# A decoder step: the down projection's middle groups in seven products, with the weights' sums made in DRAM by transfers

## The chip, the cores and the metric

The kernel is one program on one core of a Trainium2 chip. Five engines work side by side and wait for one another by semaphores: TensorE (PE, with its weight loads as PEld), VectorE (DVE), ScalarE (ACT), GpSimd (POOL) and SyncE (SP), which here only issues transfers. Sixteen DMA engines move the data between DRAM and the on-chip memory. The metric is the device time of one execution, in microseconds (us).

## The reference, cut to what matters

One layer is applied to 576 tokens (512 of a prompt and 64 of eight samples), each a vector of 1024, all in float32.

```python
h = rmsnorm(x, g_pre_mix)
z = h @ w_in                      # gated linear attention, retention, gates
m = mixers(z) @ w_mix_out         # chunked recurrences, two branches of 4 heads
x = x + rmsnorm(m, g_post_mix)
mk, mv = rmsnorm(mem) @ w_xk, rmsnorm(mem) @ w_xv     # 256 memory tokens
x = x + rmsnorm(cross_attn(rmsnorm(x), mk, mv, w_xq, w_xo), g_post_xa)
hf = rmsnorm(x, g_pre_ffn)
x = x + rmsnorm(square(relu(hf @ w_up)) @ w_down, g_post_ffn)   # hidden width 4096
```

The change is in the last line, and in what loads `x` and `mem` at the start.

## The kernel before

**Float32 in three matmuls.** Activations lie with features on the partitions and the tokens in two halves of 288 columns. Every float32 operand is split into a high part in a reduced format (`fp32r`, a ScalarE copy, L94) and a low part, the rest (a VectorE subtraction, L95); a product of two tiles takes the three matmuls high by high, low by high and high by low (L251 to L253 in `mm3`, L281 in `sevenfold`).

**Weights.** A list `plan` holds every weight tile in the order of use, 128 rows of 1024 (512 KB). `wfetch` (L172) has SP load the next one into a ring of six `wraw` buffers; `wsplit` makes `wh` and `wl` from it (rings of three); `wnext` keeps two split tiles ahead of TensorE. `gemm_m` takes one tile and makes 48 matmuls, 24 for each half of the tokens.

**Order.** First the memory's keys and values, while `xnorm` loads and normalizes the tokens; then eight mixer units, one for each head of each branch (`unit` in `mixers`): eight `gemm_m` each (q, k, two for v, four for gates), between whose halves `tick()` advances side chains written as generators: scores, attention and states of the same unit. A chain's step `attend` ends in a norm whose power is taken on GpSimd (`rs`, L887), and two steps later `turn` (L1029) transposes the normed tile on TensorE. Then come the output projection, the cross-attention and the feed-forward part. Each engine executes its own instructions strictly in the order in which they stand in its queue; the framework lays these orders down when the program is built, and sets the semaphore waits by the tiles that are read and written.

**Feed-forward.** The hidden width is cut into four groups `g` of 1024. Group 0 is made plainly. In groups 1 to 3 the up projection goes by `sevenfold`: for each of four blocks of 256 hidden columns the product is a 2 by 2 by 2 product of blocks (input halves, output halves, token halves), and a scheme of the Strassen and Winograd kind makes it with seven block products of 12 matmuls instead of eight. Its sums of activations (`fsh`, `fsl`) are made once, and the sums of weights by VectorE for each block (`begin`, four subtractions `minus` at L213, in the buffers of the ring and a separate buffer `wq`). The down projection of every group is plain: eight `gemm_m`, whose results are added onto `y3` (L734 copies the first group's, L761 adds the next two groups', and `last` ends with the fourth). `sevenfold`'s results pass through relu and square on ScalarE (L714 to L724) and are split into `hh` and `hl`.

Of the kernel before, what the change touches and what calls it, by code (L numbers as in the profile page):

```python
# [13 lines left out]
P = 128  # L14
# [12 lines left out]


RING, STAY, RAW, SEVEN = 0, 1, 2, 3
# [29 lines left out]
def decoder_step(ctx, tc, xT, memT, ktc, vc, s_gla, s_ret, w_in, w_ga, w_a2, w_mix, w_xq, w_xk, w_xv, w_xo,  # L59
                 w_up, w_ups, w_down, vecs, cst, gam, y_out, mk_out, mv_out, sg_p, sr_p, sg_s, sr_s):  # L60
# [122 lines left out]
    def wsplit():
        if units:
            units.pop(0)()
        elif raws:
            if raws[0][1] == SEVEN:
                begin()
                return
# [4 lines left out]
            pool = staying[-1] if mode == STAY else wp  # L194
            wh = pool.tile([P, 1024], F32R, name="wh")
            wl = pool.tile([P, 1024], F32R, name="wl")
            split(wh, wl, raw)
            ready.append((wh, wl))

    def halves(w):  # L200
        return w.rearrange("p (q n) -> p q n", q=2)

    def begin():


        while len(raws) < 2:
            wfetch()
        p0, p1 = (raws.pop(0)[0] for _ in range(2))
        t = wp.tile([P, 1024], F32, name="wraw", bufs=N_RAW)
        q0, q1, qt = halves(p0), halves(p1), halves(t)  # L210

        def minus(out, a, b):
            nc.vector.tensor_tensor(out=out, in0=a, in1=b, op=ALU.subtract)  # L213

        def ring(raw):
            wh = wp.tile([P, 1024], F32R, name="wh")
            wl = wp.tile([P, 1024], F32R, name="wl")
            split(wh, wl, raw)
            ready.append((wh, wl))

        def own(raw, o, n):
# [1213 lines left out]
```

## Time and profile before

| what | value |
|---|---|
| median of 3 runs | 1197.8 us (1197.7 to 1197.8) |
| the profiled execution's own time | 1200.96 us |
| span of the profiled execution, first to last instruction | 1199.2 us |
| TensorE busy / its weight loads | 1168.2 us (97%) / 1134.6 us (95%) |
| VectorE / ScalarE / GpSimd busy | 747.2 us / 564.1 us / 152.7 us |
| mean granted clock of TensorE | 0.99 of full speed |

Busy times of engines are shares of the span. Matmuls overlap in their pipeline, so the length of a stage, not the duration of one matmul, says what a matmul costs. Idle time of an engine that is not the bottleneck costs nothing.

### The profile page before, as it was taken

To read this page: it belongs to the slowest core of one execution; us is meant where nothing else is said; L and a number is where in the kernel's file an instruction comes from. 1 tells how busy PE (TensorE), PEld (TensorE's weight loads), DVE (VectorE), ACT (ScalarE), POOL (GpSimd) and SP (SyncE) were. 2 spreads that over 40 slices of the span, in tenths; PEclk is the share of its full clock that TensorE was granted. 3 is DMA by queue.
4 is the path that set the end of the run, shared out by engine and by line. 5 is a ranking of instruction groups with operands and counts; after the bars stand their busy time and mean duration, and the time that the engine had idled before them with its cause. 6 is when DMAs were issued, how large, how long until landed. Compare 5 with 4: busy or idle time off the path is not lost.

```text
span 1199.2 us, 22007 instructions
## 1 busy us (share of the span) xinstructions
PE 1168.2 (97%) x9022; PEld 1134.6 (95%) x9022; DVE 747.2 (62%) x1334; ACT 564.1 (47%) x993; POOL 152.7 (13%) x165
## 2 busy tenths in 40 slices
PE   8999999999999999999999989999999999999995
PEld 7899999999999999999999878889999999999995
DVE  6756657566746574757777545686937546456565
ACT  5534546443444344524564534556527416515652
POOL 0521213122312231221001000000000000000000
PEclk9999999999999999999999999999999999999998
DMA  8762424232424232422745677653223223321631
GB/s 291 244 213 89 128 80 137 75 125 88 128 71 143 74 128 89 128 89 76 231 130 159 226 233 238 222 164 123 88 71 105 89 71 103 109 71 56 217 108 60
DMA packets 65621, 157.98 MB, mean 132 GB/s; under 512 B 5648, under 2 KB 34576, under 8 KB 65392
## 3 DMA queue, kind: packets, MB, share of 16 engines
q1 hardware_dynamic: 65520, 156.57, 41.0%
q8 instruction: 71, 1.16, 0.4%
q14 instruction: 30, 0.25, 0.1%
HBM read 140.29 MB, written 16.25 MB: 131 GB/s over the span
## 4 chain that ended last, share of the span: by engine, by line
PE 89%; DVE 4%; DMA 2%; ACT 2%; issue 1%; POOL 1%; SPq 0%; POOLq 0%; DVEq 0%; ACTq 0%
PE psg L251 22%; PE psg L252 22%; PE psg L253 22%; PE psa L281 6%; PE psg L281 3%; PE psa L251 2%; PE pso L281 2%; PE psa L252 1%; PE psa L253 1%; DMA wraw<-in_w_xo 1%; PE pso L1254 1%; DVE wl L95 1%; PE psa L1097 1%; PE pso L1092 1%; DVE res L527 1%
## 5 line engine op out<-in xcount | busy, mean ns | idle before, releaser
L251 PE MATMUL psg<-xh,wh 128*128 128x288 f32 x1280 | 381.5, 298 | 0.4 <-DVE t L819 0.3
L252 PE MATMUL psg<-xh,wl 128*128 128x288 f32 x1280 | 377.9, 295 | 0.8 <-DVE wl L95 0.8
L253 PE MATMUL psg<-xl,wh 128*128 128x288 f32 x1280 | 377.8, 295 | 0.0
L95 DVE TENSOR_TENSOR wl<-wraw,wh 128x1024 fp32r<-128x1024 f32 x196 | 241.8, 1234 | 93.0 <-ACT wh L94 92.3
L94 ACT CAST wh<-wraw 128x1024 fp32r<-128x1024 f32 x196 | 206.0, 1051 | 187.5 <-PE psg L253 105.7
L251 PEld LDWEIGHTS psg<-xh,wh 128*128 128x128 f32 x1280 | 240.8, 188 | 3.5 <-issue 2.2
L252 PEld LDWEIGHTS psg<-xh,wl 128*128 128x128 f32 x1280 | 240.9, 188 | 1.1 <-DVE wl L95 1.0
L253 PEld LDWEIGHTS psg<-xl,wh 128*128 128x128 f32 x1280 | 240.6, 188 | 0.1
L251 PE MATMUL psg<-hh,wh 128*128 128x288 f32 x512 | 152.2, 298 | 0.7 <-DVE y L761 0.6
L252 PE MATMUL psg<-hh,wl 128*128 128x288 f32 x512 | 150.6, 295 | 0.3 <-DVE wl L95 0.3
L253 PE MATMUL psg<-hl,wh 128*128 128x288 f32 x512 | 150.7, 295 | 0.0
L251 PEld LDWEIGHTS psg<-hh,wh 128*128 128x128 f32 x512 | 96.1, 188 | 1.6 <-issue 1.1
L252 PEld LDWEIGHTS psg<-hh,wl 128*128 128x128 f32 x512 | 96.0, 188 | 0.6 <-DVE wl L95 0.6
L253 PEld LDWEIGHTS psg<-hl,wh 128*128 128x128 f32 x512 | 96.1, 188 | 0.0
L333 POOL TENSOR_TENSOR rs<-ms,mhalf 96x3 f32<-96x3 f32 (+1 forms) x11 | 11.0, 999 | 525.1 <-DVE ms L326 525.1
L955 ACT COPY vt<-psg 128x512 f32<-128x512 f32 x16 | 9.4, 587 | 77.5 <-PE psg L253 77.5
L887 POOL TENSOR_TENSOR rs<-mv,mhalf 128x1 f32<-128x1 f32 x48 | 29.8, 621 | 112.7 <-DVE mv L882 64.6
L957 DVE COPY vd<-psg 128x128 f32<-128x128 f32 x32 | 7.8, 286 | 55.6 <-ACT vt L955 55.6
L251 PE MATMUL psg<-bh,wh 128*128 128x288 f32 x128 | 38.4, 300 | 1.6 <-ACT wh L94 1.1
L252 PE MATMUL psg<-fh,wl 128*128 128x288 f32 x128 | 38.9, 304 | 1.0 <-DVE wl L95 1.0
L655 DVE TENSOR_TENSOR y<-psg,y 128x576 f32<-128x576 f32 x16 | 12.1, 757 | 44.4 <-PE psg L253 44.4
L251 PE MATMUL psg<-fh,wh 128*128 128x288 f32 x128 | 39.0, 305 | 0.2 <-ACT fh L94 0.2
(331 smaller groups left out, 2413.0 us busy)
## 6 DMA issues: line engine op xcount, KB each, us to landing
wraw<-in_w_in SPq DMA_DIRECT2D x64, 512.0 KB, 3.7
wraw<-in_w_down SPq DMA_DIRECT2D x38, 512.0 KB, 4.3
wraw<-in_w_ups SPq DMA_DIRECT2D x24, 512.0 KB, 3.7
wraw<-in_ktc SPq DMA_DIRECT2D x16, 512.0 KB, 5.0
wraw<-in_vc SPq DMA_DIRECT2D x16, 512.0 KB, 4.5
wraw<-in_w_xq SPq DMA_DIRECT2D x14, 512.0 KB, 4.3
wraw<-in_w_xo SPq DMA_DIRECT2D x14, 512.0 KB, 6.4
wraw<-in_w_up SPq DMA_DIRECT2D x14, 512.0 KB, 4.5
```

Source lines behind the costliest of these rows:

```text
L94: nc.scalar.copy(hi, src)
L95: nc.vector.tensor_tensor(out=lo, in0=src, in1=f32(hi), op=ALU.subtract)
L251: nc.tensor.matmul(out, ah, bh, start=first, stop=False)
L252: nc.tensor.matmul(out, al, bh, start=False, stop=False)
L253: nc.tensor.matmul(out, ah, bl, start=False, stop=last)
L281: nc.tensor.matmul(out, s[:, q, k], m[:, k], start=first and k == i == 0, stop=k == 3 and i == 2, skip_group_check=True)
L527: nc.vector.tensor_tensor(out=res[:, kk, c], in0=y[:, kk], in1=rj, op=ALU.add)
L655: nc.vector.tensor_tensor(out=out, in0=a, in1=b, op=op)
L887: nc.gpsimd.tensor_tensor(out=rs[:t], in0=mv[:t], in1=mhalf[:t, 0:1], op=ALU.pow)
L1092: nc.tensor.matmul(so[32 * j:32 * j + 8, o], qsd[:, b * 8:b * 8 + 8], s0[:, j], start=False, stop=True, skip_group_check=True, tile_positi ...
L1097: nc.tensor.matmul(U[:, j * 256:(j + 1) * 256], kst[g][:, 2 * bp + j, :], vst[g], start=True, stop=True)
L1254: nc.tensor.matmul(acc[rows, :256], x(h), w[:, h], start=first, stop=last, skip_group_check=True, tile_position=(0, 32 * h))
```

## The change

It has three parts.

1. In groups 1 and 2 the down projection too goes by `sevenfold`, in four blocks of seven products (argument `xh7`). For that the hidden activations are kept as `ha` (two quarters), `fh[:, 2]` (one) and four sums of quarters that the new `pairs` makes after each block of the up projection. In the first block of each down projection the product `A12` is taken second (`late`). The two hidden groups' results are added to `y3` in two pieces for each block.
2. The sums of weights are no longer made by VectorE. Twenty blocks (twelve of up, eight of down) take them from tensors in DRAM, `t_sev`, which transfers issued by GpSimd fill while the mixers run: for each of ten pairs of blocks four copies and four transfers that add onto what lies there, 512 KB each. `sums(after)` is called four times in each of the eight units, 32 times in all, and at ten of the calls (`SUMS_AT`) a pair is begun: a GpSimd copy `pace` reads a tile of that place (`kf`, `vt` or `G`), and two transfers of four bytes write it into the pair's tensors, so that the pair's first copies can't start before that place; the steps after it follow at the next calls (`SUM_STEPS`). A block of weights is now loaded as three raw blocks and four sums, seven pieces of 256 KB in four buffers, where two loads of 512 KB stood. `begin`, `minus`, `units` and `wq` go; the last piece has a pool of its own (`wdp`).
3. At the start the loads of the memory's tokens (`mf`, four of 256 KB) and of x (`xf`, eight of 288 KB) are issued by ScalarE instead of SP.

```diff
-RING, STAY, RAW, SEVEN = 0, 1, 2, 3
+RING, STAY, RAW, LAST = 0, 1, 2, 3
+N_SEV = 20
+
+SUMS_AT = (2, 5, 7, 10, 12, 15, 17, 20, 22, 25)
+SUM_STEPS = (0, 0, 1, 1, 2, 3, 4, 5)
 
-    def seven(w, b0):
-        return [(w[b0 + b][:, kh], SEVEN) for b in range(4) for kh in range(2)]
+    def seven(b0):
+
+        out = []
+        for n in range(b0, b0 + 4):
+            g, i = n // 2, n % 2
+            b = [w_sev[q, n] for q in range(4)]
+            t1, t2, t4 = t_sev[g]
+            out += [((b[0], t1[i]), RING), ((t2[0, i], t2[1, i]), RING), ((b[2], b[3]), RING), ((t4[i],), LAST)]
+        return out
...
     plan += whole(w_up) + rest(whole(w_up), 0) + whole(w_down)
     for g in range(1, 4):
-        plan += seven(w_ups, 4 * (g - 1))
-        plan += whole(w_down, 4 * g) + (rest(whole(w_down, 12), 0) if g == 3 else [])
+        plan += seven(8 * (g - 1))
+        plan += seven(8 * g - 4) if g < 3 else whole(w_down, 4) + rest(whole(w_down, 4), 0)
+
+
+    steps = {}
+    for g, at in enumerate(SUMS_AT):
+        b11, b12, b21, b22 = (w_sev[q, 2 * g:2 * g + 2] for q in range(4))
+        t1, t2, t4 = t_sev[g]
+        for n, (dst, src, plus) in zip(SUM_STEPS, (
+                (t1, b11, 0), (t2[1], b12, 0), (t1, b12, 1), (t2[1], b22, 1),
+                (t2[0], t1, 0), (t2[0], b22, 1), (t4, t2[0], 0), (t4, b21, 1))):
+            steps.setdefault(at + n, []).append((dst, src, plus))
+    clock = [0]
+    pace = perm.tile([1, 1], F32, name="pace")
+
+    def sums(after):
+
+        if clock[0] in SUMS_AT:
+            t1, t2, _ = t_sev[SUMS_AT.index(clock[0])]
+            nc.gpsimd.tensor_copy(pace, after[0:1])
+            for t in (t1[0], t2[1, 0]):
+                nc.gpsimd.dma_start(out=t[0:1, 0:1], in_=pace)
+        for dst, src, plus in steps.pop(clock[0], ()):
+            nc.gpsimd.dma_start(out=dst, in_=src, max_dma_last_dim=8192, **({"accum_op": ALU.add} if plus else {}))
+        clock[0] += 1
...
     def wfetch():
-        if plan and sum(m == SEVEN for _, m in raws) < 2:
+        if plan:
             src, mode = plan.pop(0), RING
-            if isinstance(src, tuple):
+            if isinstance(src, tuple) and isinstance(src[1], int):
                 src, mode = src
             raw = wp.tile([P, 1024], F32, name="wraw", bufs=N_RAW)
-            nc.sync.dma_start(out=raw if len(src.shape) == 2 else raw.rearrange("p (k n) -> p k n", n=src.shape[2]), in_=src)
+            if isinstance(src, tuple):
+                for i, t in enumerate(src):
+                    nc.sync.dma_start(out=raw[:, i * 512:(i + 1) * 512], in_=t)
+            else:
+                nc.sync.dma_start(out=raw if len(src.shape) == 2 else raw.rearrange("p (k n) -> p k n", n=src.shape[2]), in_=src)
             raws.append((raw, mode))
...
+        if raws:
             raw, mode = raws.pop(0)
...
+            n = 512 if mode == LAST else 1024
+            pool = wdp[0] if mode == LAST else staying[-1] if mode == STAY else wp
+            wh = pool.tile([P, n], F32R, name="wh")
+            wl = pool.tile([P, n], F32R, name="wl")
+            split(wh, wl, raw[:, :n])
             ready.append((wh, wl))
...
-        units.extend([unit_a, lambda: ring(t), lambda: own(p1, 0, 1024),
-                      lambda: minus(q1[:, 0], q1[:, 0], qt[:, 0]), lambda: own(q1[:, 0], 2048, 512)])
-        minus(qt[:, 1], q1[:, 1], q0[:, 1])
-        minus(q0[:, 1], q0[:, 1], q0[:, 0])
-        minus(qt[:, 0], q1[:, 1], q0[:, 1])
-        wfetch()
+        wsplit()
...
-    def sevenfold(x, p1, p5, u2, c11, c22, c12, c21):
+    def sevenfold(x, c1, c2, done1, done22, done21, late=False):
...
+        def c11():
+            prod(b, wb, 0, "A12", True)
+            add(c1[:, 0], b, c1[:, 0])
+
         prod(acc, wa, 0, "A11", True)
-        p1(acc)
-        while units:
-            wsplit()
+        nc.scalar.copy(c1[:, 0], acc)
+        if late:
+            c11()
+        prod(c, wa, 1, "S1", True)
+        nc.scalar.copy(c2[:, 1], c)
+        wmore()
         wd = ready.pop(0)
-        prod(c, wa, 1, "S1", True)
-        p5(c)
-        if raws and raws[0][1] == SEVEN:
-            begin()
         prod(acc, wc, 0, "S2", False)
-        wsplit()
-        u2(acc)
-        prod(b, wb, 0, "A12", True)
-        more()
-        c11(b)
+        nc.scalar.copy(c1[:, 1], acc)
+        wmore()
+        prod(c, wb, 1, "S4", False)
+        add(c1[:, 1], c, c1[:, 1], ALU.subtract)
         prod(acc, wc, 1, "S3", False)
-        c22(acc)
-        prod(c, wb, 1, "S4", False)
-        c12(c)
-        more()
+        add(c2[:, 1], c2[:, 1], acc, ALU.subtract)
+        done22()
+        wmore()
+        if not late:
+            c11()
+        done1()
+        wmore()
         prod(acc, wd, 0, "A22", False)
-        more()
-        c21(acc)
+        done21(acc)
+
+    def add(out, a, b, op=ALU.add):
+        nc.vector.tensor_tensor(out=out, in0=a, in1=b, op=op)
...
-            nc.sync.dma_start(out=mf[:, k:k + 2], in_=memT[:, k:k + 2])
+            nc.scalar.dma_start(out=mf[:, k:k + 2], in_=memT[:, k:k + 2])
...
-                    nc.sync.dma_start(out=xf[:, k:k + 2, hc(half)], in_=xT[:, k:k + 2, hc(half)])
+                    nc.scalar.dma_start(out=xf[:, k:k + 2, hc(half)], in_=xT[:, k:k + 2, hc(half)])
...
+    def pairs(c1, c2, sh, sl):
+
+        add(c2[:, 1], c2[:, 0], c2[:, 1], ALU.subtract)
+        add(c2[:, 0], c1[:, 0], c2[:, 0], ALU.subtract)
+        split(sh[:, 2:4], sl[:, 2:4], c2)
+        add(c1[:, 0], c2[:, 1], c1[:, 0], ALU.subtract)
+        add(c1[:, 1], c1[:, 1], c1[:, 0])
+        split(sh[:, 0:2], sl[:, 0:2], c1)
...
+        plain = g in (0, 3)
+        ha = None if plain else biga.tile([P, 2, 2, 4, NH], F32R, name="ha", tag="biga")
+
+        def xh7(n):
+            if n in SQ:
+                return hh[:, SQ[n]], hl[:, SQ[n]]
+            return (fh[:, 2], fl[:, 2]) if n == "A22" else (ha[:, 0, n == "A12"], ha[:, 1, n == "A12"])
...
-            wq.append(biga.tile([P, 4608], F32R, name="wq", tag="biga"))
...
             for k in range(KT):
-                ps = gemm_m(quarters(hh, hl), None)
-                y = h2(y3[:, k, :])
-                if g == 0:
-                    nc.scalar.copy(y, ps)
-                else:
-                    add(y, ps, y)
+                nc.scalar.copy(h2(y3[:, k, :]), gemm_m(quarters(hh, hl), None))
                 tick()
             drain()
+            continue
+
+        for b in range(4):
+            c1, c2 = (hp.tile([P, 2, NH], F32, name="hr") for _ in range(2))
+
+            def relu2(c, ps=None):
+                nc.scalar.activation(c, c if ps is None else ps, AF.Relu)
+                nc.scalar.activation(c, c, AF.Square)
+
+            def done22():
+                relu2(c2[:, 1])
+                if not plain:
+                    split(fh[:, 2, b], fl[:, 2, b], c2[:, 1])
+
+            def done1():
+                relu2(c1)
+                split(*((hh[:, 0:2, b], hl[:, 0:2, b]) if plain else (ha[:, 0, :, b], ha[:, 1, :, b])), c1)
+
+            def done21(ps):
+                relu2(c2[:, 0], ps)
+                if plain:
+                    split(hh[:, 2:4, b], hl[:, 2:4, b], c2)
+                else:
+                    pairs(c1, c2, hh[:, :, b], hl[:, :, b])
+
+            sevenfold(xf7, c1, c2, done1, done22, done21)
+        if plain:
+            break
+        for b in range(4):
+            c1, c2 = (hp.tile([P, 2, NH], F32, name="hr") for _ in range(2))
+            y = [y3[:, 2 * b:2 * b + 2, hc(half)] for half in range(2)]
+
+            def done21(ps):
+                nc.scalar.copy(c2[:, 0], ps)
+                add(y[1], y[1], c2)
+
+            sevenfold(xh7, c1, c2, lambda: add(y[0], y[0], c1), lambda: None, done21, b == 0)
...
+            sums(kf[:, 511:512])
+            sums(vt[:, 1, 511:512])
+            sums(G[:, 1, NT - 1:])
+            sums(G[:, 1, NT - 1:])
...
     def sevens(w):
-        return np.ascontiguousarray(w.reshape(4, 2, P, -1, 2, P).transpose(3, 2, 1, 4, 0, 5).reshape(-1, P, 2, KT, P))
+        return w.reshape(4, 2, P, -1, 2, P).transpose(1, 4, 3, 2, 0, 5).reshape(4, -1, P, 512)
...
-        "w_up": blocks(wu[:, :1024]), "w_ups": sevens(wu[:, 1024:]),
-        "w_down": np.concatenate([blocks(wd[g * 1024:(g + 1) * 1024]) for g in range(4)]),
+        "w_up": blocks(wu[:, :1024]),
+        "w_sev": np.concatenate([sevens(wu[:, 1024:2048]), sevens(wd[1024:2048]), sevens(wu[:, 2048:3072]),
+                                 sevens(wd[2048:3072]), sevens(wu[:, 3072:])], axis=1),
+        "w_down": np.concatenate([blocks(wd[:1024]), blocks(wd[3072:])]),
...
+    t_sev = [[nc.dram_tensor(f"t_sev{g}{i}", s + [2, P, 512], F32, kind="Internal").ap() for i, s in enumerate(([], [2], []))]
+             for g in range(N_SEV // 2)]
```

## Rows read from the trace of the kernel before

**Rows 1.** The page's first part: busy us, share of the span, instructions.

```profile
PE 1168.2 (97%) x9022; PEld 1134.6 (95%) x9022; DVE 747.2 (62%) x1334; ACT 564.1 (47%) x993; POOL 152.7 (13%) x165
```

**Rows 2.** Busy time by stage: mixers, group 1 up, group 1 down.

```profile
core 0: us, PE busy (x) PEld busy (x) DVE busy (x) ACT busy (x) POOL busy (x), PEclk, DMA share, GB/s
84.00:560.00 476.00, 475.24 (x3718) 465.52 (x3717) 296.08 (x684) 208.47 (x419) 109.80 (x113) 1.00 0.33 103
...
893.19:938.57 45.38, 45.23 (x339) 44.86 (x338) 29.64 (x39) 30.00 (x51) 0.00 (x0) 1.00 0.37 117
938.57:989.73 51.16, 51.16 (x387) 51.02 (x386) 23.98 (x28) 11.65 (x15) 0.00 (x0) 1.00 0.20 62
```

**Rows 3.** TensorE's waits, mixers and last 320 us: us in total, times, longest.

```profile
PE psa L969 <- ACT T L1008: 0.8, 1, 0.8
...
PE psg L251 <- DVE y L761: 0.6, 1, 0.6
```

**Rows 4.** The chain that ended last, group 1 up: start, us, one product.

```profile
894.78 1.60 PE psg L281 x12
```

**Rows 5.** Groups by line in one block of group 1 up, 904 to 915 us.

```profile
L213 DVE TENSOR_TENSOR wraw<-wraw 128x512 f32<-128x512 f32 x4 | 2.7, 686 | 0.0
...
L95 DVE TENSOR_TENSOR wl<-wraw,wh 128x1024 fp32r<-128x1024 f32 x2 | 2.4, 1222 | 0.6 <-ACT wh L94 0.6
...
L94 ACT CAST wh<-wraw 128x1024 fp32r<-128x1024 f32 x2 | 2.1, 1056 | 2.7 <-PE psa L281 2.7
...
L95 DVE TENSOR_TENSOR hl<-hr,hh 128x576 fp32r<-128x576 f32 x2 | 1.4, 756 | 0.9 <-ACT hh L94 0.9
...
L94 ACT CAST hh<-hr 128x576 fp32r<-128x576 f32 x2 | 1.2, 666 | 0.0
...
L718 ACT ACTIVATE hr<-hr 128x576 f32<-128x576 f32 x1 | 0.7, 687 | 0.4 <-DVE hr L655 0.4
...
L655 DVE TENSOR_TENSOR hr<-psa,hr 128x288 f32<-128x288 f32 x1 | 0.5, 457 | 0.5 <-PE psa L281 0.5
...
L727 ACT COPY hr<-psg 128x288 f32<-128x288 f32 x1 | 0.4, 402 | 0.0
```

**Rows 6.** Groups by line on VectorE, group 1 down.

```profile
L655 DVE TENSOR_TENSOR y<-psg,y 128x576 f32<-128x576 f32 x7 | 5.3, 757 | 20.3 <-PE psg L253 20.3
```

**Rows 7.** Groups by line on GpSimd, whole execution.

```profile
L887 POOL TENSOR_TENSOR rs<-mv,mhalf 128x1 f32<-128x1 f32 x48 | 29.8, 621 | 112.7 <-DVE mv L882 64.6 <-DVE mv L885 38.4 <-DVE mv L884 9.7
L1140 POOL TENSOR_TENSOR G<-G,t 128x576 f32<-128x576 f32 x14 | 20.1, 1436 | 19.9 <-ACT t L1139 19.9
...
L1149 POOL TENSOR_TENSOR merged<-merged,G 128x576 f32<-128x576 f32 x6 | 12.8, 2146 | 2.1 <-DVE G L1148 2.1
```

**Rows 8.** In order of time, one step of a unit: attention's end, power, transposes.

```profile
240.16 0.27 PE L253 MATMUL psa<-Sl,qh 128*128 128x256 f32 x1
...
243.29 0.56 POOL L887 TENSOR_TENSOR rs<-mv,mhalf 128x1 f32<-128x1 f32 x1 [1.64 <-DVE mv L885]
...
249.69 0.38 PE L1029 MATMUL psa<-idn,on 128*128 128x128 f32 x2
```

**Rows 9.** DMA in the mixers (84 to 560 us): queue, then issues, us to landing.

```profile
q1 hardware_dynamic: 25549, 48.31, 32.3%
...
wraw<-in_w_in SPq DMA_DIRECT2D x54, 512.0 KB, 3.7
```

**Rows 10.** DMA in the first 20 us, the same columns.

```profile
DMA packets 3107, 6.25 MB, mean 312 GB/s; under 512 B 408, under 2 KB 1688, under 8 KB 3107
...
q1 hardware_dynamic: 3107, 6.25, 88.9%
```

**Rows 11.** In order of time, the start: SP's two loads, ScalarE's first read.

```profile
1.72 1.85 SPq L379 DMA_DIRECT2D mf<-in_memT  x4
...
9.48 2.98 SPq L405 DMA_DIRECT2D xf<-in_xT  x4
...
18.03 0.68 ACT L349 ACTIVATE ss<-xf 128x576 f32<-128x576 f32 x1
```

More of the change, by code (lines that the diff above doesn't have):

```diff
@@ L59, in decoder_step @@
 def decoder_step(ctx, tc, xT, memT, ktc, vc, s_gla, s_ret, w_in, w_ga, w_a2, w_mix, w_xq, w_xk, w_xv, w_xo,
-                 w_up, w_ups, w_down, vecs, cst, gam, y_out, mk_out, mv_out, sg_p, sr_p, sg_s, sr_s):
+                 w_up, w_sev, w_down, vecs, cst, gam, t_sev, y_out, mk_out, mv_out, sg_p, sr_p, sg_s, sr_s):
     nc = tc.nc
@@ L193, in wsplit, with wmore @@
                 return
[L194 to L197, printed above, removed]
+            n = 512 if mode == LAST else 1024
[3 more added lines that the diff above has]
+            split(wh, wl, raw[:, :n])
             ready.append((wh, wl))
[L200 to L206, printed above, removed]
+    def wmore():
+        while plan and len(raws) < N_RAW - 1:
             wfetch()
[L208 to L221, printed above, removed]
-            w = wq[0][:, o:o + n], wq[0][:, o + n:o + 2 * n]
-            split(*w, raw)
-            ready.append(w)
-        def unit_a():
-            ring(p0)
-            wfetch()
-        units.extend([unit_a, lambda: ring(t), lambda: own(p1, 0, 1024),
-                      lambda: minus(q1[:, 0], q1[:, 0], qt[:, 0]), lambda: own(q1[:, 0], 2048, 512)])
-        minus(qt[:, 1], q1[:, 1], q0[:, 1])
-        minus(q0[:, 1], q0[:, 1], q0[:, 0])
-        minus(qt[:, 0], q1[:, 1], q0[:, 1])
-        wfetch()
+        wsplit()
     def wnext(n=P):
         while sum(len(r) == 2 for r in ready) < 2 and (raws or plan):
-            while not units and plan and len(raws) + sum(len(r) == 1 for r in ready) < N_RAW - 1:
-                n0 = len(raws)
+            while plan and len(raws) + sum(len(r) == 1 for r in ready) < N_RAW - 1:
                 wfetch()
-                if len(raws) == n0:
-                    break
-            if not raws and not units:
+            if not raws:
                 break
@@ L664, in sums_f @@
             yield
-            add(c2[:, 1], c2[:, 0], c2[:, 1])
-            add(c2[:, 0], c1[:, 0], c2[:, 0], ALU.subtract)
-            add(c1[:, 0], c2[:, 1], c1[:, 0], ALU.subtract)
-            add(c1[:, 1], c1[:, 1], c1[:, 0], ALU.subtract)
+            pairs(c1, c2, fsh[:, :, j], fsl[:, :, j])
             yield
-            split(fsh[:, 2:4, j], fsl[:, 2:4, j], c2)
-            split(fsh[:, 0:2, j], fsl[:, 0:2, j], c1)
-            yield
-    FQ = {"A11": (fh, fl, 0), "A12": (fh, fl, 1), "A22": (fh, fl, 3),
-          "S2": (fsh, fsl, 0), "S4": (fsh, fsl, 1), "S3": (fsh, fsl, 2), "S1": (fsh, fsl, 3)}
+    SQ = {"S2": 0, "S4": 1, "S3": 2, "S1": 3}
     def xf7(n):
-        h, l, q = FQ[n]
-        return h[:, q], l[:, q]
+        return (fsh[:, SQ[n]], fsl[:, SQ[n]]) if n in SQ else tuple(
+            t[:, {"A11": 0, "A12": 1, "A22": 3}[n]] for t in (fh, fl))
     y3 = None
@@ L783, in mixers @@
     e = Env(env)
-    nc, split, split_p, gtile, atile, gemm_m, mm3, f32, h2, tick, side = (
-        e.nc, e.split, e.split_p, e.gtile, e.atile, e.gemm_m, e.mm3, e.f32, e.h2, e.tick, e.side)
+    nc, split, split_p, gtile, atile, gemm_m, mm3, f32, h2, tick, side, sums = (
+        e.nc, e.split, e.split_p, e.gtile, e.atile, e.gemm_m, e.mm3, e.f32, e.h2, e.tick, e.side, e.sums)
     ident, vec, mhalf, merged, xh, xl = e.ident, e.vec, e.mhalf, e.merged, e.xh, e.xl
```

41 lines of the change are left out of this document (7 added, 34 removed).

## The prediction

> **What bounds the kernel now.** I read the page's first part, then the stages, then TensorE's waits, the chain and the groups by line. TensorE is busy 97% of the span, VectorE 62%, ScalarE 47%, GpSimd 13% [rows 1]. A busy matmul may still be waiting in its pipeline, so I look at where TensorE stands idle. In the mixers it is idle for 0.76 of 476 us, and in the two stages of feed-forward group 1 for 0.15 of 45.38 and 0.00 of 51.16 us [rows 2]. The waits say the same: one of 0.8 us in the mixers, one of 0.6 us in the later part shown [rows 3]. So in all the stages that the change touches, but for the start, the number of matmuls sets the time. Fewer matmuls are worth their whole length there, and anything that makes TensorE wait costs its whole length.
>
> **What is saved.** One product of 12 matmuls takes 1.60 us of the chain [rows 4], 0.133 us a matmul; the plain down projection agrees: 8 tiles of 48 matmuls are 384, and 51.16 / 384 = 0.133 us [rows 2]. By sevens a down projection has 4 x 7 x 12 = 336 matmuls, 44.8 us instead of 51.2. Two groups save 2 x 6.4 = **12.8 us**. Group 2's stages have the shape of group 1's (one pair of stages is shown of two).
>
> **What the seven products need of the other engines.** In a block of up, now, VectorE does four subtractions of weights (2.7 us), low parts of 3.5 weight tiles (3.5 x 1.22 = 4.3), two low parts of 576 columns (1.4) and three additions of 288 (3 x 0.46 = 1.4): 9.8 us in a block of 7 x 1.60 = 11.2 [rows 4, 5]. The change takes off the 2.7 and puts on, in groups 1 and 2, `pairs` (four additions of 288, 1.84, and two low parts of 576 in place of one, 0.76) and the low part of `fh[:, 2]` (0.46): 9.8 - 2.7 + 3.1 = 10.2 us. ScalarE has 3.5 high parts (3.7), hidden high parts (2 x 0.67), three copies (1.2) and the relus and squares (about 2.9): 9.1 us; it gains a high part of 576 and one of 288 and pays four short activations where some were joined, about 1.2 us: 10.3 us [rows 5]. Both stay below 11.2, so I cost eight such blocks at little, 0.5 us in all; the cover is 0.9 us a block, and if it is gone each block gets longer by what is missing. In a block of down VectorE has 4.3 + 3 x 0.46 + 2 x 0.76 = 7.2 us against about 6 plain tiles' worth before, ScalarE 3.7 + 4 x 0.4 = 5.3 us [rows 5, 6]: hidden.
>
> **The seam from up to down, twice.** The last up block ends with `A12` and `A22`. Say `A22` ends at 0. `A12`'s sum is ready at -1.6 + 0.46 = -1.1; relu, square and high part (0.69 + 0.67 + 0.67) end at +0.9, the low part (0.76) at +1.7 [rows 5]. Down's `A11` wants block 3 after nine matmuls, at +1.2: a stall of 0 to 0.5 us. The second product there is `A12` again, and its weights `wb` sit in a ring slot that the last up `A12` freed at -1.6; their high part (1.05) queues behind `done1` and ends at about +2.0, the low part (1.22) at +3.3, where TensorE wants it at about +1.9. That is 1 to 2 us of stall at a seam. What is late next is `pairs` of block 3 (about +5.6), which product `S1` wants at about +6: just in time. Bounds 0 and 3 us; I take 1.5, as the high part's place in ScalarE's order decides: **+3.0 us** for two seams.
>
> **Loads in the feed-forward part.** A block of sevens loads 7 x 256 KB = 1.84 MB in 11.2 us, 164 GB/s, where it was 117 [rows 2]. The start moves 312 GB/s [rows 10]. Five buffers in flight are over 15 us ahead of their use, a load lands in 3.7 us [rows 9]. Nothing on the path; SP issues seven instead of two a block.
>
> **The sums in the mixers: transfers.** 80 transfers of 512 KB are 41.9 MB, beside 48.3 MB that take 32.3% of the engines' time over 476 us [rows 9], so about 312 GB/s fills them, as at the start [rows 10]. No transfer from DRAM to DRAM stands in the trace. One pass each is 134 us, +0.28 of the 476; reading and writing counted apart (two passes for 40 copies, three for 40 additions: 200 x 0.524 / 312) is 336 us, +0.71, which with 0.33 is full. I take copies as one pass and additions as two, +0.42, in all 0.75, since the loads on chip also read and write at once. Then w_in's 3.7 us grow, but tiles are fetched five ahead, 6.4 us each.
>
> **The sums in the mixers: GpSimd's queue.** It gets 100 issues and 10 copies in 32 calls, three or four a call. No issue from GpSimd is shown; the shortest regular piece of its work is 0.62, the longest 2.15 us [rows 7], so 62 to 215 us on top of its 110 of 476 [rows 2], or 2 to 7 us a call; at ten of them the `pace` transfers must land first (nearest row 3.7 us [rows 9]). I take 1 us an issue: it is little arithmetic, like the power. Behind a call on this in-order queue stand the powers of the norms, for which VectorE and then TensorE's transposes wait. The slack: attention ends at 240.4, the power at 243.85, the transposes start at 249.69 [rows 8], 5.8 us with one VectorE operation in between. A call of 3 to 5 us is hidden behind this. Bounds 0 and 34 us (10 us a call, 4.2 over the slack, at one call in each of eight units); I take **+1.5 us**.
>
> The Trainium skill speaks against this part: SBUF — State Buffer, section "SBUF: two separate sides", says that while VectorE runs an operation that takes both ports, GpSimd can't write the descriptors of its transfers. The rows point the same way: the same addition of 128 x 576 takes GpSimd 1.44 us at L1140 and 2.15 at L1149, where it runs beside VectorE's additions [rows 7], a factor 1.5. By the one an issue stays 1 us and a call 3 to 4; by the other 1.5 us and 5 to 6, the edge of the slack. It is the second rival's mechanism.
>
> **The start.** ScalarE takes over 12 issues. SP's four for `mf` take 1.85 us, four for `xf` 2.98 [rows 11]. The weights behind them come up to 1.9 us sooner, but the DMA engines are 88.9% busy there [rows 10], so they come at `mf`'s expense. x was issued at 9.48 and first read at 18.03 [rows 11]; issued later by ScalarE, in order behind its splits, it may be some us late. Bounds -1 and +3; I take **+0.5**.
>
> **Sum.** -12.8 + 0.5 + 3.0 + 1.5 + 0.5 = -7.3 us. The profiled execution's own 1200.96 us would be 1193.7; it lies 3.2 above the median of 1197.8, which becomes **1190.5 us**. Its own range, with seams, blocks and start at their bounds, is 1185 to 1195.4.
>
> **Rivals.**
> 1. ScalarE becomes the bound in the sevens. For: 10.3 of 11.2 us with hand-overs to VectorE both ways. Against: 9.1 and 9.8 us ran with no idle TensorE [rows 2]. If each of the eight up blocks takes 1 us more, or the seams and start stand at their upper ends, the sum is 1198: no change.
> 2. Slower: GpSimd's queue is held in the mixers. For: the factor of 1.5 above, and a step that waits for its predecessor to land holds all behind it. Against: 5.8 us of slack, and calls 12 us and more apart. It decides once a call takes about 7 us: over 1.2 us at 8 units is 10 us, 1200.5; at 10 us a call it is 34 us, 1224.
> 3. Slower: the DMA engines fill up, because additions count three passes. Then 336 + 157 = 493 us of transfers in 476: +17 us, 1207, and state loads come late besides.
> 4. The products are not fewer in effect, because the seams eat them: 6.4 us at each would be needed against the 3 bounded above. Hardly.
>
> **Chances.** Forecast 0.66, rival 1 0.13, rival 2 0.13, rival 3 0.06, rival 4 0.02. A measurement tells 0.2%, 2.4 us, from no change. Faster: the forecast and a fourth of rival 1, 0.69; same: the rest of rival 1 and rival 4, 0.11; slower 0.20. The range 1184.5 to 1203 leaves out the worse ends of rivals 2 and 3 and a gain nearly whole.
>
> **What will show it.** The stages of down in groups 1 and 2 should be 45 to 47 us long; a 51 there refutes the saving. At the seams TensorE should wait for `wl` or `ha` by 1 to 2 us. In the mixers TensorE's idle time should stay under 3 us; if it waits at L1029 or L969, with GpSimd's queue busy or waiting for `t_sev`, rival 2 holds; if it waits for `wh` behind loads and the DMA share is above 0.9, rival 3. Idle TensorE within the up blocks behind ScalarE is rival 1. The prediction is wrong if the mixers get longer by over 5 us, or the start by over 3.

## The result

The changed kernel takes 1208.4 us (median of 4 runs, 1206.4 to 1211.0) where the kernel before, run beside it, takes 1197.8 (1197.7 to 1200.2): a ratio of 1.0074, 95% interval 1.0058 to 1.0090. It is slower by 0.7%. The forecast was 1190.5, faster, in a range that ends at 1203. The profiled execution took 1210.95 us, with a span of 1209.2.

The page of the changed kernel, from its busy times and its DMA queues, answers to [rows 1]. TensorE has 96 instructions fewer and is busy for 4.6 us less; GpSimd is busy for 65 us more and has a DMA queue of its own, q0.

```profile
PE 1163.6 (96%) x8926; PEld 1126.1 (93%) x8926; DVE 769.2 (64%) x1374; ACT 595.6 (49%) x1069; POOL 217.5 (18%) x275
...
q1 hardware_dynamic: 77168, 168.89, 43.6%
q0 software_dynamic: 7040, 41.95, 15.1%
```

The stages of the changed kernel follow, cut at TensorE's first product on each stage's input: mixers, the middle, group 0, then group 1's up and down by themselves, and all from the first seven products to the end. They answer to [rows 2].

```profile
core 0: us, PE busy (x) PEld busy (x) DVE busy (x) ACT busy (x) POOL busy (x), PEclk, DMA share, GB/s
67.30:592.60 525.30, 510.06 (x3952) 494.15 (x3952) 320.80 (x712) 219.19 (x438) 178.42 (x228) 0.99 0.66 182
592.60:807.90 215.30, 208.68 (x1687) 193.82 (x1686) 136.36 (x220) 111.24 (x197) 13.15 (x20) 0.99 0.62 200
807.90:915.30 107.40, 105.42 (x786) 103.97 (x785) 69.01 (x98) 53.43 (x74) 2.56 (x2) 1.00 0.43 129
915.51:960.11 44.60, 44.60 (x336) 44.60 (x336) 33.56 (x52) 33.89 (x62) 0.00 (x0) 1.00 0.48 148
960.11:1004.96 44.85, 44.85 (x334) 44.31 (x333) 29.83 (x42) 23.44 (x39) 0.00 (x0) 1.00 0.52 165
915.30:1209.20 293.90, 280.41 (x2082) 277.27 (x2080) 196.81 (x279) 172.80 (x298) 1.69 (x2) 0.98 0.49 153
```

The kernel before, cut in the same way:

```profile
65.70:569.00 503.30, 502.16 (x3953) 489.98 (x3952) 311.87 (x712) 219.84 (x438) 113.24 (x118) 1.00 0.34 108
569.00:784.10 215.10, 208.48 (x1688) 193.69 (x1687) 136.28 (x220) 111.34 (x197) 13.16 (x20) 0.99 0.63 201
784.10:893.00 108.90, 106.92 (x786) 105.49 (x785) 76.64 (x109) 54.16 (x75) 2.56 (x2) 0.98 0.38 118
893.00:1199.20 306.20, 292.78 (x2178) 289.60 (x2176) 176.72 (x228) 140.22 (x221) 1.69 (x2) 0.98 0.32 99
```

So the part with the seven products gained 306.2 - 293.9 = 12.3 us, and the down stage of group 1 takes 44.85 us with TensorE never idle, where plain products took 51.16 [rows 2]. The mixers lost 525.3 - 503.3 = 22.0 us with the same matmuls in them. The start is 1.6 longer, the middle 0.2 longer, group 0 1.5 shorter: 1.6 + 22.0 + 0.2 - 1.5 - 12.3 = +10.0, the difference of the spans. Group 0's 1.5 is no gain of the change: in this execution of the kernel before the granted clock was 0.98 there. The whole question is the mixers.

There TensorE was idle for 1.1 us before and for 15.2 now. Of the 7.9 us more in which it counts as busy, the granted clock accounts for some: it is 0.83 in two stretches of 10 us, in each of which a wait of TensorE of over 2 us ends.

```profile
310.00:320.00 10.00, 9.28 (x57) 8.11 (x58) 7.48 (x20) 2.12 (x6) 1.26 (x3) 0.83 0.91 234
370.00:380.00 10.00, 7.45 (x49) 6.87 (x50) 8.22 (x17) 5.01 (x13) 5.06 (x6) 0.83 0.89 243
```

A mean of 0.83 between the levels 2.4 and 1.2 GHz is 3.4 us at the lower one, so 1.7 us of work lost each time, 3.4 in all. The other 4.5 us of the longer busy time I did not break down.

The changed kernel's waits in the mixers (us in total, times, longest) show the chain; [rows 3] had one wait of TensorE there, of 0.8 us:

```profile
POOL t_sev L201 <- DMA t_sev<-in_w_sev: 82.0, 23, 7.5
POOL t_sev L201 <- DMA t_sev<-t_sev: 52.6, 17, 5.3
DVE on L914 <- POOL rs L910: 18.5, 18, 4.8
DVE on L916 <- POOL rs L910: 17.1, 18, 5.0
POOL t_sev L201 <- DMA t_sev<-pace: 13.5, 8, 3.2
PE psa L1142 <- DVE on L916: 5.1, 2, 3.0
PE psa L1122 <- DVE on L914: 2.9, 2, 2.3
PE psa L994 <- DVE vl L98: 2.7, 1, 2.7
```

In order of time, one such case (start, us, engine, instruction, and in brackets its idle time and who ended it):

```profile
308.70 0.79 POOL L201 DMA_DIRECT2D t_sev<-in_w_sev  x1 [5.22 <-DMA t_sev<-t_sev]
309.27 0.82 POOL L910 TENSOR_TENSOR rs<-mv,mhalf 128x1 f32<-128x1 f32 x1
310.12 0.54 DVE L914 TENSOR_SCALAR on<-psa,ag,rs 128x256 f32<-128x256 f32 x1 [4.84 <-POOL rs L910]
...
310.72 0.56 PE L1122 MATMUL psa<-vs,ks 128*128 128x256 f32 x2 [2.29 <-DVE on L914]
```

GpSimd stands 5.22 us at a transfer that may not start before the transfer ahead of it has landed. Behind it in its queue is the power of a norm, whose input had been ready since 304.1. VectorE waits 4.84 us for the power, and TensorE 2.29 us for VectorE to give back the accumulator. Such waits come in rows, because the compiled order has the later steps of a group together, where the program has them a call (some 16 us on average) apart; GpSimd alone, earlier:

```profile
219.64 0.52 POOL L201 DMA_DIRECT2D t_sev<-t_sev  x1 [4.16 <-DMA t_sev<-in_w_sev]
225.10 0.78 POOL L201 DMA_DIRECT2D t_sev<-in_w_sev  x1 [4.93 <-DMA t_sev<-t_sev]
230.94 0.53 POOL L201 DMA_DIRECT2D t_sev<-t_sev  x1 [5.07 <-DMA t_sev<-in_w_sev]
```

Three of TensorE's four waits of over 2 us (2.29, 2.96 and 2.10 us) come so, through a power. The fourth comes through another small instruction of GpSimd, the masking of the scores `sm`, which stands behind a transfer held for 7.47 us and the next group's paced writes:

```profile
364.02 0.54 POOL L201 DMA_DIRECT2D t_sev<-t_sev  x1 [7.47 <-DMA t_sev<-in_w_sev]
...
366.09 0.31 POOL L1003 TENSOR_SCALAR_AFFINE_SELECT sm<-sm 128x128 f32<-128x128 f32 x1
366.43 0.30 ACT L97 CAST sh<-sm 128x128 fp32r<-128x128 f32 x1 [4.28 <-POOL sm L1003]
...
372.55 0.80 PE L994 MATMUL psa<-qf,kf 128*128 128x128 f32 x2 [2.71 <-DVE vl L98]
```

ScalarE waits 4.28 us for the mask, VectorE 4.22 for ScalarE, and `vl`, further back in both queues, comes late.

The issuing itself is cheap, as its group by line says:

```profile
L201 POOL DMA_DIRECT2D t_sev<-in_w_sev x60 | 43.5, 741 | 87.0 <-DMA t_sev<-t_sev 52.6 <-DMA t_sev<-in_w_sev 20.4 <-DMA t_sev<-pace 13.5
```

And the transfers around it, 84 to 560 us, against [rows 9]:

```profile
q0 software_dynamic: 7040, 41.95, 38.3%
q1 hardware_dynamic: 24512, 46.54, 30.2%
wraw<-in_w_in SPq DMA_DIRECT2D x55, 512.0 KB, 4.8
```

### The profile page after: what moved, and what is told of

It reads as the page before. It is cut to its first block, busy times and chain, and to the rows that moved or that the text cites. A ratio compares the mean times of both kernels' runs of the same rounds, so it can differ in the third digit from the quotient of the medians.

```text
span 1209.2 us, 22374 instructions
## 1 busy us (share of the span) xinstructions
PE 1163.6 (96%) x8926; PEld 1126.1 (93%) x8926; DVE 769.2 (64%) x1374; ACT 595.6 (49%) x1069; POOL 217.5 (18%) x275
## 4 chain that ended last, share of the span: by engine, by line
PE 74%; DMA 8%; DVE 8%; issue 4%; POOL 3%; ACT 3%; POOLq 0%; DVEq 0%; SPq 0%; ACTq 0%
PE psg L251 15%; PE psg L252 15%; PE psg L250 15%; PE psa L280 11%; PE psg L280 5%; DMA t_sev<-in_w_sev 3%; PE pso L280 3%; DMA t_sev<-t_sev 2%; DVE wl L98 2%; PE psa L250 1%; PE psa L251 1%; PE psa L252 1%; ACT wh L97 1%; DMA wraw<-in_w_xo 1%; PE pso L1281 1%
## 5 line engine op out<-in xcount | busy, mean ns | idle before, releaser
L98 DVE TENSOR_TENSOR wl<-wraw,wh 128x1024 fp32r<-128x1024 f32 (+1 forms) x236 | 286.8, 1215 | 117.4 <-ACT wh L97 114.3
L97 ACT CAST wh<-wraw 128x1024 fp32r<-128x1024 f32 (+1 forms) x236 | 239.1, 1014 | 149.0 <-PE psg L252 55.9
L250 PE MATMUL psg<-hh,wh 128*128 128x288 f32 x256 | 75.7, 296 | 0.7 <-DVE y L784 0.6
L251 PE MATMUL psg<-hh,wl 128*128 128x288 f32 x256 | 75.6, 296 | 0.3 <-DVE wl L98 0.3
L252 PE MATMUL psg<-hl,wh 128*128 128x288 f32 x256 | 75.5, 296 | 0.0
L201 POOL DMA_DIRECT2D t_sev<-in_w_sev x60 | 43.5, 741 | 87.0 <-DMA t_sev<-t_sev 52.6
L250 PEld LDWEIGHTS psg<-hh,wh 128*128 128x128 f32 x256 | 48.1, 188 | 1.2 <-issue 1.1
L251 PEld LDWEIGHTS psg<-hh,wl 128*128 128x128 f32 x256 | 48.1, 188 | 0.6 <-DVE wl L98 0.6
L252 PEld LDWEIGHTS psg<-hl,wh 128*128 128x128 f32 x256 | 48.0, 188 | 0.2 <-DVE hl L98 0.2
L252 PE MATMUL psg<-bl,wh 128*128 128x288 f32 x128 | 38.6, 301 | 0.0
```

The costliest lines, as they stand in the source:

```text
L97: nc.scalar.copy(hi, src)
L98: nc.vector.tensor_tensor(out=lo, in0=src, in1=f32(hi), op=ALU.subtract)
L201: nc.gpsimd.dma_start(out=dst, in_=src, max_dma_last_dim=8192, **({"accum_op": ALU.add} if plus else {}))
L250: nc.tensor.matmul(out, ah, bh, start=first, stop=False)
L251: nc.tensor.matmul(out, al, bh, start=False, stop=False)
L252: nc.tensor.matmul(out, ah, bl, start=False, stop=last)
```

## The experiments

Twelve kernels ran. Two theories of the 22 us were open after the profile: the *queue* (GpSimd held by chained transfers, and its time to issue), and the *traffic* (42 MB more in the mixers make loads and stores late). In this table "mixers" runs from TensorE's first product there to its first product on `bh`, all in us; the ratio is to the kernel before on the same chip. The mixers are read from the one profiled execution of a kernel, which can lie some us from its median (held_rs 1198.7 against 1202.2, changed 1210.95 against 1208.4), so a difference of 3 us in that column says little.

| kernel | mixers | time, median | ratio (95%) |
|---|---|---|---|
| before | 503.3 | 1197.8 | 1 |
| changed | 525.3 | 1208.4 | 1.0074 (1.0058 to 1.0090) |
| no_sums | 503.3 | 1188.2 | 0.9912 (0.9896 to 0.9929) |
| apart_held | 518.7 | 1204.9 | 1.0048 (1.0025 to 1.0070) |
| held | 519.0 | 1201.3 | 1.0026 (1.0008 to 1.0044) |
| sp_loads | 529.5 | 1209.2 | 1.0074 (1.0048 to 1.0101) |
| held_sn4 | 509.0 | 1194.1 | 0.9957 (0.9941 to 0.9972) |
| small | 506.0 | 1191.6 | 0.9937 (0.9922 to 0.9953) |
| act_copies | 535.1 | 1223.0 | 1.0186 (1.0157 to 1.0215) |
| rs_dve | 510.3 | 1196.8 | 0.9973 (0.9957 to 0.9990) |
| after_sn4 | 527.8 | 1212.2 | 1.0097 (1.0062 to 1.0132) |
| held_sn4_sp | 512.1 | 1194.1 | 0.9957 (0.9943 to 0.9971) |
| before_act | 502.4 | 1199.3 | 0.9999 (0.9990 to 1.0008) |
| held_rs | 516.3 | 1202.2 | 1.0026 (1.0011 to 1.0041) |

**No sums at all.**

```diff
-            sums(kf[:, 511:512])            # and the three other calls
-            out += [((b[0], t1[i]), RING), ((t2[0, i], t2[1, i]), RING), ((b[2], b[3]), RING), ((t4[i],), LAST)]
+            out += [((b[0], b[1]), RING), ((b[2], b[3]), RING), ((b[2], b[3]), RING), ((b[1],), LAST)]
```

> The changed kernel without the transfers of the sums (no call of sums in the mixers); the blocks of seven products load raw weights in place of the sums, so what is computed there is not the reference's. The stages compared: up to the first mixer matmul 71.3 us, mixers 521.3, sevens and the end 293.9. Both theories of the mixers (the wait on GpSimd's queue; the transfers' traffic) expect the mixers back at 499 to 500 us and the whole at 1185 to 1188 us; if the mixers stay above 505 us, the loss has another source than the sums.

The mixers are back at 503.3 us to the tenth, and the time is 0.9% under before. (The text counts the mixers from the first product of a `gemm_m`, 4.0 us later than the table; by that count they take 499.3.) Everything lost comes with the sums; the rest of the change together saves 11.2 us by the medians, about what the seven products save.

**The same transfers, none waiting for another.**

```diff
-                (t1, b11, 0), (t2[1], b12, 0), (t1, b12, 1), (t2[1], b22, 1),
-                (t2[0], t1, 0), (t2[0], b22, 1), (t4, t2[0], 0), (t4, b21, 1))):
+                (t1, b11, 0), (t2[1], b12, 0), (apart[g, 0], b12, 1), (apart[g, 1], b22, 1),
+                (apart[g, 2], b11, 0), (apart[g, 3], b22, 1), (apart[g, 4], b12, 0), (apart[g, 5], b21, 1))):
...
-            nc.gpsimd.dma_start(out=dst, in_=src, ...)
+            tc.keep_in_program_order(nc.gpsimd.dma_start(out=dst, in_=src, ...))
```

> The same 80 transfers of the sums, copies and additions of 512 KB, at the places of their calls, but 60 of them write to places of their own, so that none waits for another to land; the blocks load raw weights, so what is computed there is not the reference's. Queue theory (GpSimd stands waiting for a predecessor's landing): mixers 500 to 506 us, the whole 1187 to 1193. Traffic theory (DMA engines shared, weights and states late): mixers stay at 515 to 522 us, the whole 1203 to 1209.

The chained waits are gone, and the mixers still take 518.7 us. My first reading, that the held queue is the whole loss, fell here: 15 us come even when no transfer waits for another. But the edit changes two things, the chaining and the order of the transfers; the next has the order alone.

**The sums as they are, kept in the program's order.** By itself the scheduler had moved the later steps of several groups forward and together; here each stays in its call.

```diff
-            nc.gpsimd.dma_start(out=dst, in_=src, ...)
+            tc.keep_in_program_order(nc.gpsimd.dma_start(out=dst, in_=src, ...))
```

> The changed kernel with every transfer of the sums kept in GpSimd's queue behind the instructions that stand before its call in the program; nothing else. Queue theory: its predecessor, 12 us and more earlier, has mostly landed, the waits on t_sev fall from some 135 us to under 50, mixers 503 to 511 us, the whole 1190 to 1198. Traffic theory: no change, 1206 to 1210.

6.3 us come back, under a third of the loss, which neither theory gave: the waits on `t_sev` fall as the queue theory had it, from 148 us to 34.5, and the mixers don't follow. The waits of this kernel name what takes the place of the rest: an engine that was in no theory, VectorE, waiting for the store of the sampled states, `sn`, to leave its buffer.

```profile
POOL t_sev L201 <- DMA t_sev<-in_w_sev: 26.8, 8, 6.0
DVE sn L1130 <- DMA out_sgs<-sn: 7.5, 2, 5.2
PE psa L1054 <- DVE on L916: 6.0, 2, 5.0
```

In order of time, the longer of the two:

```profile
381.70 1.08 POOL L910 TENSOR_TENSOR rs<-mv,mhalf 128x1 f32<-128x1 f32 x2 [3.11 <-DVE mv L908]
...
388.82 0.69 DVE L1130 TENSOR_TENSOR sn<-s,psa 128x512 f32<-128x512 f32 x1 [5.17 <-DMA out_sgs<-sn]
...
389.52 1.19 DVE L98 TENSOR_TENSOR wl<-wraw,wh 128x1024 fp32r<-128x1024 f32 x1
390.62 0.48 DVE L916 TENSOR_SCALAR on<-psa,rs 128x256 f32<-128x256 f32 x1
...
391.25 0.66 PE L1054 MATMUL psa<-idn,on 128*128 128x128 f32 x2 [5.00 <-DVE on L916]
```

`rs` had been there since 382.8. VectorE, in order, could not reach `on`, because an addition into `sn` stood ahead of it, and its buffer was still being stored. TensorE lost 5.0 us, and the ten microseconds in which the wait ended have a granted clock of 0.67:

```profile
390.00:400.00 10.00, 8.75 (x50) 8.78 (x51) 5.09 (x13) 2.91 (x8) 3.09 (x5) 0.67 0.40 132
```

**Memory's tokens and x back on SP.**

```diff
-            nc.scalar.dma_start(out=mf[:, k:k + 2], in_=memT[:, k:k + 2])
+            nc.sync.dma_start(out=mf[:, k:k + 2], in_=memT[:, k:k + 2])
...
-                    nc.scalar.dma_start(out=xf[:, k:k + 2, hc(half)], in_=xT[:, k:k + 2, hc(half)])
+                    nc.sync.dma_start(out=xf[:, k:k + 2, hc(half)], in_=xT[:, k:k + 2, hc(half)])
```

> The changed kernel with the memory's tokens and x loaded by SP again. If ScalarE's issues are what makes the start longer, the first mixer matmul is at 69.5 to 70 us instead of 71.3 and the whole 1206 to 1207.5 us; if not, the whole stays at 1208 to 1209. The mixers stay at 519 to 523 us by every theory.

The first product of the mixers comes at 66.5 us (67.3 in the changed kernel, 65.7 before), and the time does not move. By the text's own count it comes at 70.5, half a microsecond above the range given for SP, and the mixers take 525.5, above the 519 to 523 that every theory gave.

The next four were to tell the two theories apart, with the store of `sn` now named.

**Four buffers for `sn` in held.**

```diff
-                        sn = u2.tile([P, 2, 256], F32, name="sn")
+                        sn = u2.tile([P, 2, 256], F32, name="sn", bufs=4)
```

> The kernel held (all transfers for the sums in the program's order on GpSimd's queue), with four buffers in place of two for sn, the updated states that VectorE writes and a store takes away. Store theory: under the sums' traffic the stores of sn land late (3.5 us before, 5.0 in held), VectorE waits for a free sn (7.5 us in two waits, the longest 5.2) and everything behind it on VectorE, the normalised outputs that TensorE transposes among it, comes late; with two more buffers the mixers take 506 to 512 us (519.0 in held) and the time is 1188 to 1195 us. Issue theory: what costs is GpSimd's own work of issuing (its busy time in the mixers rises from 114 to 176 us), so the buffers change nothing: mixers 517 to 521 us, time 1199 to 1203 us.

The mixers fall by 10.0 us to 509.0, and the kernel is 0.4% faster than before (1194.1 against 1199.3). Of the 10.0 the medians show 7.2 (1201.3 to 1194.1): in the profiled executions the mixers begin 1.3 us later than in held and the middle is 2.1 longer. No store of `sn` is waited for any more, although one now takes 7.5 us to land (5.0 in held, 3.5 before). TensorE's waits there are 3.3 us in all, the longest two:

```profile
PE psg L250 <- DVE qs L957: 1.6, 2, 0.9
PE psa L994 <- ACT T L1033: 0.7, 1, 0.7
```

**As many transfers, a sixteenth of the bytes.**

```diff
+            tc.keep_in_program_order(nc.gpsimd.dma_start(out=dst[0, 0:64, 0:128], in_=src[0, 0:64, 0:128], ...))
```

> The kernel apart_held, with each of its 80 transfers cut to 64 rows of 512 bytes (32 KB in place of 512 KB): GpSimd issues as many transfers at the same places, with as many rows, and a sixteenth of the bytes moves. The sums are left out (the products use raw blocks). Issue theory: the mixers take 512 to 519 us as in apart_held (518.7). Store theory (traffic): 503 to 506 us as without any sums (503.3), and VectorE waits for no store of sn; time 1187 to 1191 us.

506.0 us, the upper end of what the traffic theory gave. GpSimd issues all it did in apart_held and is as busy (177.9 against 176.9 us in the mixers), so 2.7 of apart_held's 15.4 us are the issuing and 12.7 the bytes.

**The same bytes from ScalarE.**

```diff
-            tc.keep_in_program_order(nc.gpsimd.dma_start(out=dst, in_=src, ...))
+            tc.keep_in_program_order(nc.scalar.dma_start(out=dst, in_=src, max_dma_last_dim=8192))
```

> The kernel apart_held, with the 80 transfers issued by ScalarE in place of GpSimd, all as plain copies of 512 KB to places of their own, and without the two tiny paced writes ahead of each group: the same 42 MB written and a third less read, and GpSimd has nothing of it. The sums are left out (the products use raw blocks). Traffic theory: mixers 511 to 520 us, with VectorE waiting for stores of sn as in apart_held (9.6 us). Issue theory: 503 to 507 us, GpSimd's queue being as before the change.

535.1 us, which neither theory gave. GpSimd is as free as before the change (108.5 us busy), and VectorE waits 4.8 us for a store of `sn`; but ScalarE now has the transfers among its own work, and the trace puts 5.3 us of its idle time down to one of them landing. So a loss comes with none of the transfers on GpSimd too, but through other waits; it does not say where the changed kernel's comes from, and as a measure of the traffic alone it failed.

**The power taken off GpSimd in the changed kernel.**

```diff
-            nc.gpsimd.tensor_tensor(out=rs[:t], in0=mv[:t], in1=mhalf[:t, 0:1], op=ALU.pow)
+            nc.vector.tensor_tensor(out=rs[:t], in0=mv[:t], in1=mhalf[:t, 0:1], op=ALU.mult)
```

> The changed kernel, with one instruction taken off GpSimd: the power in the mixers' normalisation is replaced by a product on VectorE (so the normalised values are not the reference's; the work and order of all else stays). Queue theory: in the changed kernel a chained transfer holds GpSimd's in-order queue up to 7.5 us, the power behind it comes late and TensorE waits 8 us for the normalised outputs, at a lower clock after; without the power there the mixers take 510 to 517 us (525.3 in the changed kernel) and VectorE has no long wait for GpSimd. Store theory alone: 520 to 526 us, the waits moving to VectorE's stores.

510.3 us, 15.0 less than the changed kernel. GpSimd is held for even longer than there, and most of the loss is gone; the wait that comes through `sm` is still there:

```profile
POOL t_sev L201 <- DMA t_sev<-in_w_sev: 119.4, 30, 8.2
POOL t_sev L201 <- DMA t_sev<-t_sev: 61.2, 19, 6.9
...
PE psa L994 <- DVE vl L98: 2.6, 1, 2.6
```

So in the profiled executions 15 of the 22 us pass through this one small instruction behind the transfers; by the medians of the whole kernel it is 11.6 us (1208.4 to 1196.8). In the kernel before TensorE was idle for only 1.1 us of the mixers, so the edit had little to win but what the transfers had cost.

**Four buffers for `sn` in the changed kernel.** The edit is that of held_sn4, with the order left free.

> The changed kernel itself (its order of transfers left free) with four buffers for sn. In its trace VectorE waits for a store of sn once, 0.9 us, while VectorE waits 35 us for the power on GpSimd behind held transfers. If the changed kernel's loss is the held queue: mixers 522 to 526 us (525.3), time 1204 to 1210 us. If late stores were its cause as in held: 510 to 515 us, time 1193 to 1199 us.

527.8 us: no gain, a little outside the range given, on the side away from late stores. The changed kernel waits 0.9 us for its stores, and buffers can't mend what stands in GpSimd's queue.

**The power taken off GpSimd in held.** The edit is that of rs_dve, on held.

> The kernel held with the power of the mixers' normalisation replaced by a product on VectorE (so the normalised values are not the reference's): GpSimd's queue can hold no norm any more, and sn keeps its two buffers. Store theory: held's loss is VectorE's wait for late stores of sn, which does not pass through GpSimd, so the mixers stay at 515 to 520 us (519.0 in held) with the wait of some 5 us near 385 us still there. Queue theory: what is left of the chained waits in held (26.8 us in eight waits) is the loss: 506 to 511 us.

516.3 us, and VectorE waits for stores longer than in held:

```profile
DVE sn L1130 <- DMA out_sgs<-sn: 14.7, 4, 5.6
```

With the order kept, then, the power's place is worth at most 2.7 us (by the medians nothing: 1202.2 against held's 1201.3), where it was worth 15.0 in the free order; the buffers are worth 10.0 in the one and nothing in the other. The two causes are separate, and which of them sets the time depends on the order of the transfers.

**The two parts that concern the start.** held_sn4_sp is held_sn4 with the edit of sp_loads; before_act is the kernel before with ScalarE in SP's place at those two lines.

> The kernel held_sn4 with the loads of memory's tokens and of x put back on SP's queue. The start theory: with ScalarE issuing them the first product of the mixers begins 1.6 to 2.4 us later than before (65.7 us), and on SP again 0.8 us later (66.5 in sp_loads); time 1192 to 1194 us against 1194.05 of held_sn4, 0.5% under the kernel before. If the queue of those loads is of no account: 1193.5 to 1195.5 us.

> The kernel before with that one part of the change alone: memory's tokens and x loaded by ScalarE. If ScalarE's issuing is what delays the start: the first product of the mixers at 66.7 to 67.5 us (65.7 before), time 1200 to 1201.5 us. If the delay of the changed kernel's start comes from elsewhere (the no_sums kernel with the same loads began at 66.8): 65.5 to 66.2 us and no difference in time.

The first product of the mixers moves (65.8 us where 66.5 was expected, and 67.0), but their end hardly does: 577.9 against 577.1 us in held_sn4, 569.4 against 569.0 before. The times are those of held_sn4 within 0.1 us and of before within 0.1%. The mixers make up a late first product, so who issues these loads is of no account, and a length in the table's column holds up to 3 us of an early or late start (509.0 and 512.2 us for these two). The Trainium skill (DMA: Bandwidth & Descriptors, section "Issuing engines are not separate DMA queues") says that transfers of all issuing engines run on the same 16 DMA engines, and that issuing from several engines saves only the time that a sequencer takes to issue; the ratio of 0.9999 agrees.

## Why the prediction was wrong

**The saving** of 12.8 us was right: 12.3 measured, and 44.60 and 44.85 us for the stages of group 1 against 44.8 computed.

**The seams** (+3.0) and the up blocks (+0.5) were too dear: the saving left after them is 12.3 of 12.8, so they cost 0.5 together. From 912 us to the end TensorE waits for nothing that it did not wait for before. The 45 to 47 us given for down was pessimistic (44.85), and rival 1, ScalarE as the bound, did not come.

**The start** (+0.5) costs nothing measurable, as before_act shows.

**The transfers** fill 38.3 + 30.2 = 68.5% of the DMA engines in the mixers, where I had 75%: rival 3 did not come, and weights landed in 4.8 us instead of 3.7, without being waited for. But I followed the traffic to the weights alone. Rival 3 names late loads of states, without a price; their stores were left out, and `sn` has two buffers. The changed kernel hardly pays for that (0.9 us); its improved version, held, does.

**The step that failed is the term for GpSimd's queue, +1.5 us; with the start, +23.6 stood there at the end of the mixers.** I priced a call by what its issues cost, three to five at 1 us, and held it against a slack of 5.8 us. The issues do cost 0.74. What I left out of the sum is that a step of a chain may not be issued before the step ahead has landed, 7.0 us for a copy from the weights, and that GpSimd stands still until then: 148 us in 48 waits, the longest 7.5. The clause is in rival 2 word for word ("a step that waits for its predecessor to land holds all behind it"), with the point from which it decides, 7 us a call. I gave it 0.13 and 1200.5 to 1224 us; 1208.4 is what it looks like. I took it for granted that the steps of a chain stay a call apart, as the program has them; there a landing would be over, and in held, which enforces it, 9 chained waits are left. Had I taken them to be drawn together, two landings of [rows 9]'s 3.7 us make a call of over 7, the point from which this rival decides. The rule of the Trainium skill that I weighed there (SBUF — State Buffer, section "SBUF: two separate sides") would have made an issue longer; at 0.74 us a mean it was not what held the queue. Undoing it two ways agrees: without the power in the queue 15.0 us come back, with the order kept 6.3, and in the second case a new wait takes part of the gain (16.3 come back with four buffers for `sn` besides). Of the signs named for rival 2 the wait at L969 came (now L994, 2.7 us, behind `sm`), and the transposes that waited for the powers were those of the samples (L1142).

Some workings are off beside that. The seams and the start at their upper ends give 1196.0, where the prediction has 1195.4 for its own range and 1198 in rival 1. And the factor of 1.5 compares a product (L1140) with an addition (L1149), not the same addition twice: in the run small one of the additions, with VectorE idle beside most of it, takes 1.78 us against 2.15, a factor of 1.2.

**Open.** Why the free order collides so little with the stores (0.9 us of waiting, though a store lands in 5.2 us) and the kept order so much (7.5, with 5.0) was not settled; the times at which transfers and stores fall together differ, and I did not follow them one by one. Nor are the last 5.7 us of held_sn4 over 503.3 fully told: 2.7 are the issuing, by small. For those the trace has a mechanism. Before, GpSimd's two additions into `merged` ended as VectorE's subtraction began:

```profile
198.53 4.25 POOL L1149 TENSOR_TENSOR merged<-merged,G 128x576 f32<-128x576 f32 x2 [0.70 <-DVE G L1148]
...
202.43 0.97 DVE L856 TENSOR_TENSOR t<-t,t 128x576 f32<-128x576 f32 x1 [0.93 <-ACT t L854]
```

In small, issues stand ahead of them and between them, and the two engines meet:

```profile
201.72 1.78 POOL L1176 TENSOR_TENSOR merged<-merged,G 128x576 f32<-128x576 f32 x1
203.08 1.34 POOL L201 DMA_DIRECT2D t_sev<-in_w_sev  x2
203.09 3.40 DVE L879 TENSOR_TENSOR t<-t,t 128x576 f32<-128x576 f32 x1 [1.28 <-ACT t L877]
204.11 1.76 POOL L1176 TENSOR_TENSOR merged<-merged,G 128x576 f32<-128x576 f32 x1
```

The subtraction takes 3.40 us instead of 0.97, and a wait of TensorE of 0.7 us for `qs` behind it follows; the same meeting in a later unit (3.72 us) is followed by one of 1.0. held and held_sn4 have both meetings, 3.4 and 3.7 us, and where the additions end before the subtraction begins it takes 0.75. Here as before the change the subtraction ends 0.6 us after the second addition. The Trainium skill (SBUF — State Buffer, section "SBUF: two separate sides") has an instruction of VectorE with two inputs in SBUF and one of GpSimd that reads SBUF take a shared port pair as a lock for a whole instruction; a subtraction that ends only after GpSimd's addition agrees with that. Moving the calls away from the additions was not tried.

## What to carry to other kernels

A transfer that must wait for another is not free because an idle engine issues it: on an in-order queue its price is up to the landing time of the transfer ahead (waits of up to 7.5 us here), paid by whatever small instruction stands behind it. Look first for the cheapest instruction on that engine that the critical path needs. When traffic is added to a stage, go through every transfer in that stage and count its buffers, the stores above all, not the one stream that moves the most bytes; two more buffers of 2 KB a partition were worth 10 us of the mixers here, 7 of the whole. And where the scheduler may move transfers, hold their order before judging them.

## What was not expected of the hardware

A single wait of TensorE can bring the lower clock with it: for two of the changed kernel's four waits of over 2 us the ten microseconds in which they end have a granted mean of 0.83, for the 5.0 us of held one of 0.67, which by the means is 1.7 and up to 3.3 us of work on top of the waits, an estimate; after the other two the clock stayed at 1.00. A store of 256 KB took 7.5 us to land in held_sn4 where it took 3.5 before, with the DMA engines at 66% and not full. And beside GpSimd's additions of 128 x 576 VectorE's subtraction took three and a half times as long (3.40 us against 0.97).
